# The last block of rows: columns in parts of 384 and 128, squares summed on VectorE, rows stored in halves

## The chip, the cores and the metric

The kernel runs on one core of a Trainium2 chip. The metric is the device time of one execution in microseconds, lower is better. Engines are named as in the profile: PE (TensorE), DVE (VectorE), ACT (ScalarE), POOL (GpSimd), SP (SyncE, which here issues most DMAs).

## The reference

One layer of a hybrid decoder trunk: 512 tokens, model width 1024, float32. What matters here is its last part, the channel mixer's down-projection with its residual, and the final RMSNorm:

```python
u2 = _rmsnorm(h, norm2_g[l])
z = _causal_dwconv(u2 @ w_ffn_up[l], ffn_dw_w[l], ffn_dw_b[l])
h = h + (jax.nn.silu(z[..., :FFN_DIM]) * z[..., FFN_DIM:]) @ w_ffn_down[l]
...
return _rmsnorm(h, final_g)

def _rmsnorm(x, g):
    xf = x.astype(jnp.float32)
    y = xf * lax.rsqrt(jnp.mean(xf * xf, axis=-1, keepdims=True) + EPS)
    return (y * g.astype(jnp.float32)).astype(x.dtype)
```

So each output row needs the mean of the squares of all its 1024 columns before any of it can be scaled.

## The kernel before, in words

**Tiles.** The 512 tokens are four blocks of 128 rows, t = 0 to 3; the 1024 columns are two halves of T = 512, n = 0 and 1. `hres[t, n]` is the residual of one block and half in SBUF. H is 256, P is 128, D is 1024.

**Matmuls.** Every product is split into a high and a low part of each operand, so one product of 128 x 128 weights is three matmuls (`mm3`, lines 448 to 450), high and low parts being `whi`/`wlo` for the weights. The down-projection runs in the function `seven` (a Strassen-like scheme with seven products for two-by-two blocks) over three groups of channel pairs; the third group is the last work of PE. Its steps run in the order a11, a12, s1, n2, s4, n3, a22, each for the two row blocks of one half (i = 0, 1). After a step the result in PSUM is added into `hres` by VectorE (`add`, line 1419). Steps a12, s4, n3 and a22 complete a block and half: a12 completes (0, 0) and (1, 0), s4 completes (0, 1) and (1, 1), n3 completes (2, 1) and (3, 1), a22 completes (2, 0) and then (3, 0). The last to be complete is thus the first half of block 3.

**The last block in two parts.** For (a22, i = 1) in the last group (`fine`), the 512 columns are made in two parts of 256: twelve matmuls into the step's own bank for columns 0 to 256, then twelve into a new bank for 256 to 512. What the old bank holds for the second part from earlier steps is added to `hres` after n3 (line 1441). The two adds, with what they bring about, are in a region in which VectorE and ACT issue in program order; outside such a region a scheduler orders each engine's instructions by the readiness that it expects.

**The final norm.** A `Finish` object for each block collects the pieces. `part` (line 1570 on) is called when a piece of `hres` is complete: ACT squares it and sums the squares into a column of `ss4` (line 1576, two instructions: the pass and the read of the sum), VectorE multiplies it by the gain into `y` (line 1578), and the sums are added up, the first by VectorE with EPS (line 1583), later ones by POOL (line 1585). `scale` adds the last sum (POOL, line 1591) and raises it to the power -1/2 (POOL, line 1592), which gives the factor of each row. `store` scales and writes. For blocks 2 and 3 ACT scales the first 384 columns (line 1598), VectorE the other 640 (line 1599), and SP issues one store of the whole 512 KB block (line 1600). For blocks 0 and 1 ACT scales each half and SP issues two stores of 256 KB (lines 1603, 1604).

**The order around the change.** `last_complete` calls `part`, then `scale` for blocks 2 and 3 when all 1024 columns are there, and `store` for block 2 when the first part of block 3's first half has been handled, for block 3 when the second part has. `last_at` scales and stores blocks 0 and 1 at the start of a22.

Of the kernel before, what the change touches and what calls it, by code (L numbers as in the profile page):

```python
# [12 lines left out]
BF16 = mybir.dt.bfloat16  # L13
U8 = mybir.dt.uint8
AF = mybir.ActivationFunctionType
ALU = mybir.AluOpType

P = 128
D = 1024
T = 512  # L20
# [55 lines left out]
def trunk_layer(ctx: ExitStack, tc: tile.TileContext, a: dict, out: bass.AP):  # L76
    nc = tc.nc
# [23 lines left out]
    def nm(s):  # L101
        return f"{s}_{next(names)}"
# [13 lines left out]
    def small(n, tag):  # L116
        return tp.tile([P, n], F32, tag=tag, name=nm(tag), bufs=4)

    def mm_bank():
        return ps.tile([P, T], F32, tag="mm", name=nm("mm"), bufs=5)  # L120
# [14 lines left out]
    mhalf = cp.tile([P, NT], F32, name="mhalf")  # L135
# [372 lines left out]
    def junk(n):  # L508
        return tp.tile([P, n], BF16, tag="junk", name=nm("junk"), bufs=1)
# [44 lines left out]
    rows = tp.tile([P, P], F32, tag="gain", name=nm("rows"), bufs=1)[0:KT, :]  # L554
# [44 lines left out]
    def root(t):  # L599
        v = small(1, "var")  # L600
        nc.vector.tensor_scalar(v, rs[t], EPS, None, ALU.add)
        rs[t] = tp.tile([P, 1], F32, tag="r1", name=nm("r1"), bufs=NT)
        nc.gpsimd.tensor_tensor(rs[t], v, mhalf[:, :1], ALU.pow)
# [29 lines left out]
    def scale(t):  # L633
        nc.scalar.activation(xs[t], xs[t], AF.Copy, scale=rs[t])
# [95 lines left out]
    acc = mm_bank()  # L730
# [7 lines left out]
    acc = mm_bank()  # L738
# [77 lines left out]
    for k in range(KT):  # L816
# [4 lines left out]
        c = heap()  # L821
# [104 lines left out]
    rows = slice(32, 32 + RANK)  # L926
# [9 lines left out]
    rows = slice(96, 96 + RANK)  # L936
# [165 lines left out]


    H = T // 2

    def f32(x):
        return x.bitcast(F32)

    def token_sums_7(u, src, hi, lo):
# [3 lines left out]
        def part(t, k):  # L1113
            return [u[k][j][:, :, t * H : (t + 1) * H] for j in range(2)]

# [50 lines left out]
    def step_of_two(acts7, acc, step, w, half, opens):  # L1166
        ah, al = acts7[step]
        for k in range(4):
            s = slice(half * T + k * P, half * T + (k + 1) * P)
            mm3(acc[:, :H], (w[0][:, s], w[1][:, s]), (ah[k], al[k]), opens and k == 0, k == 3, not opens)  # L1170

    combined = []

    def two_tiles(name, p, q, acts7, side_bank, at_once=False):

        x, y, z = mm_bank(), side_bank(), side_bank()
        c1, c2 = tmp(), tmp()
        t1, t2 = slice(0, H), slice(H, T)

        def put(c, acc):  # L1180
            nc.scalar.copy(c, acc[:, :H])  # L1181

# [9 lines left out]
        step(z, "a12", w, 1, True)  # L1192
        combine(c1[:, t1], c1[:, t1], z[:, :H], ALU.add)
        yield
# [178 lines left out]
    def seven(name, pairs, acts, complete, at=lambda step, i: None, fine=False):  # L1373

        bank = {"x": [mm_bank(), mm_bank()], "y": [mm_bank(), mm_bank()], "z": [ax_bank(), ax_bank()]}  # L1380
        of = {"a11": "x", "n2": "x", "n3": "x", "a22": "x", "s1": "y", "s4": "y", "a12": "z"}

        into = {
            "a11": (0, 0, ALU.add, False),
            "a12": (0, 0, ALU.add, True),
            "s1": (1, 1, ALU.add, False),
            "n2": (0, 1, ALU.subtract, False),
            "s4": (0, 1, ALU.add, True),
            "n3": (1, 1, ALU.subtract, True),
            "a22": (1, 0, ALU.add, True),  # L1390
        }

        def products(step, i, parts, acc, lo=0, hi=T, opens=False):
            acc = acc[:, lo:hi]
            opens = opens or step in ("a11", "s1", "a12")
            for d, w in parts:
                for j, pair in enumerate(acts[2 * d : 2 * d + 2]):
                    ah, al = (x[:, i * P : (i + 1) * P] for x in pair[step])
                    c = slice(j * T + lo, j * T + hi)

                    read = 2 * d + j == len(acts) - 1
                    mm3(acc, (ah, al), (w[0][:, c], w[1][:, c]), opens and d == 0 and j == 0, read, not opens)

        steps = list(STEPS)
        while steps:
            step, d = steps.pop(0)

            with tc.issue_after(freed.ins) if step == "a22" and not fine else ExitStack():
                parts = [(d, weight(name, (pairs, step, d)))]
                if steps and steps[0] == (step, 1):  # L1410
                    steps.pop(0)
                    parts.append((1, weight(name, (pairs, step, 1))))
            half, n, op, whole = into[step]
            for i in range(2):
                t = 2 * half + i
                acc = bank[of[step]][i]

                def add(n, acc, c=slice(0, T)):
                    done = nc.vector.tensor_tensor(hres[t, n][:, c], hres[t, n][:, c], acc[:, c], op)  # L1419
                    if whole:  # L1420
                        complete(t, n, c)
                    return done

                if fine and (step, i) == ("a22", 1):
                    products(step, i, parts, acc, 0, H)
                    rest = mm_bank()
                    products(step, i, parts, rest, H, T, True)
                    with tc.manual_schedule(engines={ET.DVE, ET.Activation}):
                        add(n, acc, slice(0, H))
                        add(n, rest, slice(H, T))  # L1430
                    continue
                products(step, i, parts, acc)
                if parts[-1][0] == 1:
                    at(step, i)
                    done = add(n, acc)
                    if (step, i) == ("n3", 1):
                        freed = done
                if fine and (step, i) == ("n3", 1):

                    c = slice(H, T)  # L1440
                    nc.vector.tensor_tensor(hres[t, 0][:, c], hres[t, 0][:, c], acc[:, c], ALU.add)


# [1 line left out]
    hres = {}  # L1445
    ss2 = {}
# [48 lines left out]
    ffn_scope, fp = scoped("ffn", 1)  # L1495
# [63 lines left out]
        hi = {"n3": b, "s1": x, "n2": x, "s4": g}  # L1559
        return token_sums_7(u2, {step: src for step in hi}, hi, {"n3": us, "s1": us, "n2": us, "s4": x})  # L1560

    SPLIT = 5 * P

    class Finish:


        def __init__(self, t):
            self.t, self.width = t, 0
            self.y = fp.tile([P, D], F32, tag="kept", name=nm("y"), bufs=2) if t > 1 else None
            self.ss = small(4, "ss4")  # L1570
            self.parts = []

        def part(self, n, c):
            hn = hres[self.t, n][:, c]
            k = len(self.parts)
            nc.scalar.activation(junk(T)[:, c], hn, AF.Square, scale=1.0 / 32.0, accum_out=self.ss[:, k : k + 1])
            y = self.y[:, n * T + c.start : n * T + c.stop] if self.y else tmp() if self.parts else hn
            nc.vector.tensor_tensor(y, hn, gain3[:, n * T + c.start : n * T + c.stop], ALU.mult)
            self.parts.append((n, y))
            self.width += c.stop - c.start  # L1580
            if k == 0:
                self.sum = small(1, "var")
                nc.vector.tensor_scalar(self.sum, self.ss[:, 0:1], EPS, None, ALU.add)
            elif self.width < D:
                nc.gpsimd.tensor_tensor(self.sum, self.sum, self.ss[:, k : k + 1], ALU.add)

        def scale(self):

            k = len(self.parts) - 1
            self.r = small(1, "rstd")  # L1590
            nc.gpsimd.tensor_tensor(self.sum, self.ss[:, k : k + 1], self.sum, ALU.add)
            nc.gpsimd.tensor_tensor(self.r, self.sum, mhalf[:, :1], ALU.pow)

        def store(self):
            rows = slice(self.t * P, (self.t + 1) * P)
            if self.y:
                lo, hi = self.y[:, : D - SPLIT], self.y[:, D - SPLIT :]
                nc.scalar.activation(lo, lo, AF.Copy, scale=self.r)
                nc.vector.tensor_scalar(hi, hi, self.r, None, ALU.mult)
                nc.sync.dma_start(out[rows, :], self.y)  # L1600
                return
            for n, y in reversed(self.parts):
                nc.scalar.activation(y, y, AF.Copy, scale=self.r)
                nc.sync.dma_start(out[rows, n * T : (n + 1) * T], y)

    ends = {}

    def last_complete(t, n, c):
        if t not in ends:
            ends[t] = Finish(t)  # L1610
        ends[t].part(n, c)
        if ends[t].width == D and t > 1:
            ends[t].scale()
        if t == 3 and n == 0:
            ends[2 if c.start == 0 else 3].store()

    def last_at(step, i):

        if (step, i) == ("a22", 0):
            for t in range(2):  # L1620
                ends[t].scale()
            for t in range(2):
                ends[t].store()

    gain3 = None
    banks, values, units = {}, {}, {}
    third = []
    for gi, pairs in enumerate(GROUPS):
        acts = []
        if gi == 0:  # L1630
# [3 lines left out]
            for j, lo in [(j, lo) for lo in (0, H) for j in range(3)]:  # L1634
                late = {(1, 0): (KT - 1, 2), (2, 0): (MID, 3)}.get((j, lo))
                at = {late[0]: lambda t=late[1]: to_channels(normed[t], u2, t)} if late else {}
# [18 lines left out]
        for what, i, *rest in up_plan(gi):  # L1655
            if what == "tile":
                if 0 in rest[0]:
                    banks[i] = (weight("w_up", i), mm_bank())
                wt, acc = banks[i]
# [26 lines left out]
        else:  # L1686
            gain3 = load_gain("final_g")
# [91 lines left out]
```

## Time and profile before

| | |
|---|---|
| median of 3 runs | 821.92 us (821.52, 821.92, 823.87) |
| the profiled execution, its own time | 820.78 us |
| its span | 818.9 us |
| PE busy | 810.3 us (99%), 4287 matmuls |
| DVE busy | 715.6 us (87%) |
| ACT busy | 448.9 us (55%) |
| POOL busy | 148.8 us (18%) |
| chain that ended last | PE 98%, DMA 1%, the rest below 0.5% each |
| granted PE clock | 0.999 |

The span is the time from the first to the last event that the profile shows of the profiled execution; the execution's own time is 1.88 us longer. Times in the rows are us from the start of the span. A row of the timeline has start, duration, engine, line, operation, output <- inputs, shape and, in brackets, the engine's idle time ahead of it with what ended it. A row of the groups has the number of instructions after x, then busy us, the mean of one in ns, and the idle time ahead. A row of the waits has the total in us, how often, and the longest.

### The profile page before, as it was taken

The page shows a single profiled execution, that of the slowest core. Times are in us where ns is not written, and L with a number is a line of the kernel's source. Part 1 is how long each engine was busy: PE and PEld are TensorE (multiplying, and loading weights), DVE is VectorE, ACT ScalarE, POOL GpSimd, SP SyncE. Part 2 cuts the span into 40 slices and gives each one's busy share as a digit, 9 for nine tenths or more (in the row PEclk, how much of TensorE's full clock was granted, in tenths as well). Part 3 has the DMA queues.
Part 4 walks back from the last instruction along what each step waited for, and adds up shares of the span by engine and source line. Part 5 has one row for each costly group of instructions (what it writes and reads, how often), then busy time and mean ns, then how long its engine had stood idle before and what let it go on. Part 6 is the DMA issues. An engine that isn't in the chain of part 4 may idle for free.

```text
span 818.9 us, 11480 instructions
## 1 busy us (share of the span) xinstructions
PE 810.3 (99%) x4287; PEld 700.5 (86%) x4287; DVE 715.6 (87%) x1157; ACT 448.9 (55%) x666; POOL 148.8 (18%) x133
## 2 busy tenths in 40 slices
PE   9999999999999999999999999999999999999996
PEld 7888888888888889999988898898889988899885
DVE  6689999999989699885788889979965999789896
ACT  6643447656663446684444556556435663466554
POOL 2000010001000213633001000230123301622012
PEclk9999999999999999999999999999999999999999
DMA  8355572563532123223657623146642447334662
GB/s 318 104 127 144 148 188 96 130 154 104 120 97 96 49 62 109 88 78 129 206 115 220 187 71 103 52 161 166 134 137 89 144 123 167 104 103 177 158 129 102
DMA packets 30615, 106.25 MB, mean 130 GB/s; under 512 B 3464, under 2 KB 3600, under 8 KB 30560
## 3 DMA queue, kind: packets, MB, share of 16 engines
q1 hardware_dynamic: 24784, 85.34, 30.4%
q0 software_dynamic: 5760, 20.19, 14.4%
q8 instruction: 33, 0.54, 0.3%
q14 instruction: 22, 0.18, 0.1%
q10 hardware_dynamic: 16, 0.00, 0.0%
HBM read 103.42 MB, written 2.10 MB: 129 GB/s over the span
## 4 chain that ended last, share of the span: by engine, by line
PE 98%; DMA 1%; ACT 0%; DVE 0%; POOL 0%; issue 0%; POOLq 0%; SPq 0%; ACTq 0%
PE mm L448 28%; PE mm L449 28%; PE mm L450 28%; PE mm L662 3%; PE ax L450 2%; PE ax L448 2%; PE ax L449 2%; PE ax L1070 1%; PE ax L1072 1%; PE ax L1051 1%; DMA raw<-in_w_v_dram 1%; PE ax L1040 0%; PE ax L529 0%; PE ax L576 0%; PE ax L1085 0%; PE mm L933 0%
## 5 line engine op out<-in xcount | busy, mean ns | idle before, releaser
L448 PE MATMUL mm<-uh,wlo 128*128 128x512 f32 (+1 forms) x672 | 244.4, 364 | 0.0
L449 PE MATMUL mm<-ul,whi 128*128 128x512 f32 (+1 forms) x672 | 242.4, 361 | 0.0
L450 PE MATMUL mm<-uh,whi 128*128 128x512 f32 (+1 forms) x672 | 242.0, 360 | 0.0
L450 PEld LDWEIGHTS mm<-uh,whi 128*128 128x128 f32 x672 | 126.8, 189 | 19.4
L448 PEld LDWEIGHTS mm<-uh,wlo 128*128 128x128 f32 x672 | 127.0, 189 | 18.8
L449 PEld LDWEIGHTS mm<-ul,whi 128*128 128x128 f32 x672 | 127.0, 189 | 18.6
L385 ACT CAST whi<-raw 128x1024 fp32r<-128x1024 f32 x86 | 89.7, 1047 | 54.9 <-PE mm L450 28.2
L356 DVE TENSOR_TENSOR wlo<-raw,whi 128x1024 fp32r<-128x1024 f32 x80 | 93.1, 1171 | 24.4 <-ACT whi L355 20.5
L327 POOL TENSOR_TENSOR raw<-raw,raw 128x512 f32<-128x512 f32 x42 | 67.6, 1610 | 212.8 <-DVE wlo L356 130.7
L390 DVE TENSOR_TENSOR wlo<-raw,whi 128x1024 fp32r<-128x1024 f32 x70 | 92.7, 1327 | 14.1 <-ACT whi L385 14.0
L355 ACT CAST whi<-raw 128x1024 fp32r<-128x1024 f32 x80 | 76.3, 957 | 34.8 <-PE mm L450 27.2
L788 DVE SCALAR_TENSOR_TENSOR c<-h,pp,c 128x255 f32<-128x255 f32 (+14 forms) x120 | 57.5, 479 | 4.0 <-ACT c L784 3.7
L788 DVE SCALAR_TENSOR_TENSOR c<-aside,btmp,c 128x255 f32<-128x255 f32 (+14 forms) x120 | 57.5, 479 | 1.4 <-ACT c L784 1.4
L788 DVE SCALAR_TENSOR_TENSOR aside<-h,pp,aside 128x255 f32<-128x255 f32 (+6 forms) x112 | 53.7, 479 | 0.0
L355 ACT CAST whi<-kept 128x1024 fp32r<-128x1024 f32 (+1 forms) x32 | 31.8, 996 | 31.8 <-DVE kept L310 17.0
L1503 DVE SCALAR_TENSOR_TENSOR tmp<-mm,pp,tmp 128x511 f32<-128x511 f32 (+1 forms) x56 | 41.4, 742 | 4.0 <-ACT tmp L1500 3.9
L356 DVE TENSOR_TENSOR wlo<-kept,whi 128x1024 fp32r<-128x1024 f32 (+1 forms) x32 | 36.8, 1153 | 4.8 <-ACT whi L355 4.7
L1181 ACT COPY tmp<-mm 128x256 f32<-128x256 f32 x48 | 17.7, 368 | 34.4 <-PE mm L450 34.0
L1419 DVE TENSOR_TENSOR hres<-hres,mm 128x512 f32<-128x512 f32 (+1 forms) x49 | 32.3, 671 | 4.7 <-PE mm L450 3.4
L1500 ACT ACTIVATE tmp<-mm,pp 128x512 f32<-128x512 f32 x28 | 21.8, 779 | 19.0 <-PE mm L450 18.9
L387 ACT ACTIVATE wlo<-raw 128x1024 fp32r<-128x1024 f32 x16 | 16.9, 1060 | 22.1 <-PE mm L448 22.1
L1503 DVE SCALAR_TENSOR_TENSOR tmp<-tmp,pp,tmp 128x511 f32<-128x511 f32 (+1 forms) x32 | 27.8, 887 | 0.4
(347 smaller groups left out, 1767.0 us busy)
## 6 DMA issues: line engine op xcount, KB each, us to landing
raw<-in_w_up_dram SPq DMA_DIRECT2D x44, 512.0 KB, 3.5
raw<-in_w_glu_dram SPq DMA_DIRECT2D x16, 512.0 KB, 5.2
raw<-in_w_down_dram SPq DMA_DIRECT2D x15, 512.0 KB, 4.3
kept<-in_w_down_dram POOLq DMA_DIRECT2D x10, 512.0 KB, 5.9
raw<-in_w_v_dram SPq DMA_DIRECT2D x8, 512.0 KB, 5.6
raw<-in_w_qk_dram SPq DMA_DIRECT2D x8, 512.0 KB, 3.4
raw<-in_w_r_dram SPq DMA_DIRECT2D x8, 512.0 KB, 4.6
wlo<-in_w_r_dram POOLq DMA_DIRECT2D x8, 512.0 KB, 8.1
```

The costliest lines, as they stand in the source:

```text
L327: work = nc.gpsimd.tensor_tensor(out, x, y, ALU.add)
L355: nc.scalar.copy(hi, raw)
L356: two_low[:] = [nc.vector.tensor_tensor(lo, raw, hi.bitcast(F32), ALU.subtract)]
L385: nc.scalar.copy(hi, raw)
L390: pace[0] = nc.vector.tensor_tensor(lo, raw, hi.bitcast(F32), ALU.subtract)
L448: nc.tensor.matmul(acc, ll, rh, start=first, stop=False, **kw)
L449: nc.tensor.matmul(acc, lh, rl, start=False, stop=False, **kw)
L450: nc.tensor.matmul(acc, lh, rh, start=False, stop=last, **kw)
L662: nc.tensor.matmul(acc, act, ready[k // 2][wi][:, j], start=first, stop=last)
L788: nc.vector.scalar_tensor_tensor(out[:, j:], x[:, : half_t - j], w, out[:, j:], ALU.mult, ALU.add)
L1419: done = nc.vector.tensor_tensor(hres[t, n][:, c], hres[t, n][:, c], acc[:, c], op)
L1503: nc.vector.scalar_tensor_tensor(z[:, s:], acc[:, : T - s], w[j], z[:, s:], ALU.mult, ALU.add)
```

## The change

The last part of the work, from (a22, i = 1) on, is rearranged.

- Columns 0 to 384 and 384 to 512 take the place of the two parts of 256. The add after n3 that carries over the old bank covers 128 columns rather than 256.
- Block 2: the squares of its second-completed half are summed by VectorE, starting from the sum that is there (`square_onto`, one instruction that multiplies, writes the squares as bfloat16 into a new tile `last`, and sums them onto a start value). POOL's add goes, the power stays. The scaling splits at 768 columns (ACT) and 256 (VectorE), and `store` is called ahead of the two adds of block 3, inside the region in program order.
- Blocks 0 and 1: POOL adds the second sum when the piece is complete, not at a22; the power and the stores stay at a22.
- Block 3: the 384-column part is squared by ACT. The last 128 columns are squared and summed by VectorE onto the first half's sum; a VectorE add joins ACT's sum; POOL makes the power. The gain product of the 384 columns is issued behind that add. VectorE scales columns 512 to 1024, which SP stores (256 KB); VectorE multiplies the last 128 columns by factor and gain in one instruction, ACT scales the 384 columns, and SP stores columns 0 to 512 (256 KB).

```diff
+    CUT = 3 * P
...
                 if fine and (step, i) == ("a22", 1):
-                    products(step, i, parts, acc, 0, H)
+                    products(step, i, parts, acc, 0, CUT)
                     rest = mm_bank()
-                    products(step, i, parts, rest, H, T, True)
+                    products(step, i, parts, rest, CUT, T, True)
                     with tc.manual_schedule(engines={ET.DVE, ET.Activation}):
-                        add(n, acc, slice(0, H))
-                        add(n, rest, slice(H, T))
+                        at("last", i)
+                        add(n, acc, slice(0, CUT))
+                        add(n, rest, slice(CUT, T))
...
-                    c = slice(H, T)
+                    c = slice(CUT, T)
                     nc.vector.tensor_tensor(hres[t, 0][:, c], hres[t, 0][:, c], acc[:, c], ALU.add)
...
-    SPLIT = 5 * P
+    SHARE = 2 * P
...
+        def square(self, n, c, k):
+            nc.scalar.activation(
+                junk(T)[:, c], hres[self.t, n][:, c], AF.Square, scale=1.0 / 32.0, accum_out=self.ss[:, k : k + 1]
+            )
+
+        def square_onto(self, x, total):
+            of = fp.tile([P, T], BF16, tag="last", name=nm("last"), bufs=1)[:, : x.shape[-1]]
+            nc.vector.tensor_tensor_reduce(of, x, x, 1.0 / D, self.sum, ALU.mult, ALU.add, total)
+
+        def gained(self, n, c, y):
+            nc.vector.tensor_tensor(y, hres[self.t, n][:, c], gain3[:, n * T + c.start : n * T + c.stop], ALU.mult)
+
         def part(self, n, c):
+            k = len(self.parts)
+            if self.t == 3 and c.start == CUT:
+                return
             hn = hres[self.t, n][:, c]
-            k = len(self.parts)
-            nc.scalar.activation(junk(T)[:, c], hn, AF.Square, scale=1.0 / 32.0, accum_out=self.ss[:, k : k + 1])
             y = self.y[:, n * T + c.start : n * T + c.stop] if self.y else tmp() if self.parts else hn
-            nc.vector.tensor_tensor(y, hn, gain3[:, n * T + c.start : n * T + c.stop], ALU.mult)
+            if self.t == 2 and k:
+                total = small(1, "total")
+                self.square_onto(hn, total)
+                self.root(total)
+            else:
+                self.square(n, c, k)
+            if c.stop != CUT:
+                self.gained(n, c, y)
             self.parts.append((n, y))
-            self.width += c.stop - c.start
             if k == 0:
                 self.sum = small(1, "var")
                 nc.vector.tensor_scalar(self.sum, self.ss[:, 0:1], EPS, None, ALU.add)
-            elif self.width < D:
-                nc.gpsimd.tensor_tensor(self.sum, self.sum, self.ss[:, k : k + 1], ALU.add)
-
-        def scale(self):
-
-            k = len(self.parts) - 1
+            elif self.t < 2:
+                nc.gpsimd.tensor_tensor(self.sum, self.ss[:, 1:2], self.sum, ALU.add)
+
+        def root(self, total):
             self.r = small(1, "rstd")
-            nc.gpsimd.tensor_tensor(self.sum, self.ss[:, k : k + 1], self.sum, ALU.add)
-            nc.gpsimd.tensor_tensor(self.r, self.sum, mhalf[:, :1], ALU.pow)
+            nc.gpsimd.tensor_tensor(self.r, total, mhalf[:, :1], ALU.pow)
+
+        def end(self):
+
+            last, before = slice(CUT, T), slice(0, CUT)
+            total = small(2, "ss2")
+            self.square_onto(hres[3, 0][:, last], total[:, 0:1])
+            nc.vector.tensor_tensor(total[:, 1:2], total[:, 0:1], self.ss[:, 1:2], ALU.add)
+            self.root(total[:, 1:2])
+            y, r, rows = self.y, self.r, slice(self.t * P, (self.t + 1) * P)
+            self.gained(0, before, y[:, before])
+            nc.vector.tensor_scalar(y[:, T:], y[:, T:], r, None, ALU.mult)
+            nc.sync.dma_start(out[rows, T:], y[:, T:])
+            nc.vector.scalar_tensor_tensor(y[:, last], hres[3, 0][:, last], r, gain3[:, last], ALU.mult, ALU.mult)
+            nc.scalar.activation(y[:, before], y[:, before], AF.Copy, scale=r)
+            nc.sync.dma_start(out[rows, :T], y[:, :T])
 
         def store(self):
             rows = slice(self.t * P, (self.t + 1) * P)
             if self.y:
-                lo, hi = self.y[:, : D - SPLIT], self.y[:, D - SPLIT :]
+                lo, hi = self.y[:, : D - SHARE], self.y[:, D - SHARE :]
                 nc.scalar.activation(lo, lo, AF.Copy, scale=self.r)
                 nc.vector.tensor_scalar(hi, hi, self.r, None, ALU.mult)
                 nc.sync.dma_start(out[rows, :], self.y)
...
-        if ends[t].width == D and t > 1:
-            ends[t].scale()
-        if t == 3 and n == 0:
-            ends[2 if c.start == 0 else 3].store()
+        if t == 3 and c.start == CUT:
+            ends[3].end()
...
             for t in range(2):
-                ends[t].scale()
+                ends[t].root(ends[t].sum)
             for t in range(2):
                 ends[t].store()
+        if step == "last":
+            ends[2].store()
```

More of the change, by code (lines that the diff above doesn't have):

```diff
@@ L1560, in ffn_sums @@
         return token_sums_7(u2, {step: src for step in hi}, hi, {"n3": us, "s1": us, "n2": us, "s4": x})
-    SPLIT = 5 * P
+    SHARE = 2 * P
     class Finish:
         def __init__(self, t):
-            self.t, self.width = t, 0
+            self.t = t
             self.y = fp.tile([P, D], F32, tag="kept", name=nm("y"), bufs=2) if t > 1 else None
```

## The prediction

> **What bounds the kernel now.** I read the table of stages first, then the list of waits of TensorE, then the timeline of the end.
>
> ```profile
> 20.00:809.22 789.22, 789.22 (x4172) 682.17 (x4171) 698.63 (x1127) 432.35 (x638) 142.62 (x111) 1.00 0.44 125
> 809.22:812.25 3.03, 3.03 (x25) 2.82 (x23) 2.62 (x5) 1.61 (x5) 1.04 (x3) 1.00 0.00 0
> 812.25:815.00 2.75, 0.00 (x0) 0.00 (x0) 1.47 (x4) 1.35 (x4) 0.94 (x3) 1.00 0.46 191
> 815.00:818.90 3.90, 0.00 (x0) 0.00 (x0) 0.00 (x0) 0.00 (x0) 0.00 (x0) 0.74 0.33 134
> ```
>
> The columns are the stage, its length, then the busy time of PE, PEld, DVE, ACT and POOL. From 20 us on, PE is busy in all of its stage, at a granted clock of 1.00, up to 812.25. Its only idle waits lie in the first stage:
>
> ```profile
> PE mm L568 <- DVE ones L541: 1.1, 1, 1.1
> PE mm L662 <- ACT h L589: 0.8, 1, 0.8
> ```
>
> So no engine beside PE can shorten what lies ahead of 812.25. The edit reaches the last matmuls and the 818.9 - 812.25 = 6.65 us behind them. This is that end:
>
> ```profile
> 809.41 0.69 DVE L1419 TENSOR_TENSOR hres<-hres,mm 128x512 f32<-128x512 f32 x1 [0.42 <-PE mm L450]
> ...
> 811.97 0.28 PE L450 MATMUL mm<-whi,ah 128*128 128x256 f32 x1
> 812.33 0.41 DVE L1419 TENSOR_TENSOR hres<-hres,mm 128x256 f32<-128x256 f32 x1
> ...
> 812.83 0.42 ACT L1576 ACTIVATE junk<-hres 128x256 bf16<-128x256 f32 x1 [0.36 <-DVE hres L1419]
> 813.16 0.19 ACT L1576 ACTIVATION_READ_ACCUMULATOR junk<-hres 128x1 f32 x1
> 813.49 0.19 POOL L1591 TENSOR_TENSOR var<-ss,var 128x1 f32<-128x1 f32 x1 [1.03 <-ACT junk L1576]
> 813.75 0.55 POOL L1592 TENSOR_TENSOR rstd<-var,mhalf 128x1 f32<-128x1 f32 x1
> 814.34 0.61 ACT L1598 ACTIVATE y<-y,rstd 128x384 f32<-128x384 f32 x1 [0.99 <-POOL rstd L1592]
> 814.34 0.55 DVE L1599 TENSOR_SCALAR y<-y,rstd 128x640 f32<-128x640 f32 x1 [1.14 <-POOL rstd L1592]
> 814.98 0.33 SPq L1600 DMA_DIRECT2D out_dram<-y  x1
> ```
>
> One chain: the last product ends at 811.97 + 0.28 = 812.25, then come residual add, squares, POOL's add, POOL's power (the root), the scaling, and at 814.98 the issue of one 512 KB store.
>
> **The store.** Its price and that of a half are in the table of DMA issues:
>
> ```profile
> out_dram<-y SPq DMA_DIRECT2D x2, 512.0 KB, 2.6
> out_dram<-tmp SPq DMA_DIRECT2D x2, 256.0 KB, 2.1
> ```
>
> The old one lands at 814.98 + 2.6 = 817.58; 1.3 us of closing follow, which I take as fixed. The new last store is of 256 KB: 2.1 from its issue, a gain of 0.5. It is issued behind its twin, though, on SP's queue (an issue takes 0.33), so they share the wire; if the pair costs what 512 KB do, it is 2.6. I take 2.1, the row of its own size, and keep 2.6.
>
> **Durations.** The groups kept apart by shape:
>
> ```profile
> L1419 DVE TENSOR_TENSOR hres<-hres,mm 128x512 f32<-128x512 f32 x47 | 31.4, 681 | 4.7 <-PE mm L450 3.4 <-DMA hres<-in_x_dram 1.2
> L1419 DVE TENSOR_TENSOR hres<-hres,mm 128x256 f32<-128x256 f32 x2 | 0.8, 418 | 0.0
> L1578 DVE TENSOR_TENSOR y<-hres,gain 128x512 f32<-128x512 f32 x3 | 2.1, 689 | 0.1
> L1578 DVE TENSOR_TENSOR y<-hres,gain 128x256 f32<-128x256 f32 x2 | 0.9, 428 | 0.1
> L1467 DVE SCALAR_TENSOR_TENSOR un<-hres,rstd,gain 128x512 f32<-128x512 f32 x8 | 5.6, 747 | 1.8 <-POOL rstd L500 1.8
> L1599 DVE TENSOR_SCALAR y<-y,rstd 128x640 f32<-128x640 f32 x2 | 1.1, 554 | 1.3 <-POOL rstd L1592 1.1
> L1583 DVE TENSOR_SCALAR var<-ss 128x1 f32<-128x1 f32 x4 | 0.6, 151 | 1.1 <-ACT junk L1576 1.1
> L1576 ACT ACTIVATE junk<-hres 128x512 bf16<-128x512 f32 x7 | 4.4, 628 | 5.5 <-DVE hres L1419 5.5
> L1576 ACT ACTIVATE junk<-hres 128x256 bf16<-128x256 f32 x2 | 0.8, 418 | 0.8 <-DVE hres L1419 0.8
> L1576 ACT ACTIVATION_READ_ACCUMULATOR junk<-hres 128x1 f32 x9 | 1.7, 187 | 0.0
> L1603 ACT ACTIVATE tmp<-tmp,rstd 128x512 f32<-128x512 f32 x2 | 1.4, 720 | 1.1 <-POOL rstd L1592 1.1
> L1598 ACT ACTIVATE y<-y,rstd 128x384 f32<-128x384 f32 x2 | 1.2, 616 | 1.0 <-POOL rstd L1592 1.0
> ```
>
> On straight lines through two widths: residual add 128 columns 0.29, 384 columns 0.55; gain product 128 columns 0.30, 384 columns 0.56; tensor_scalar 512 columns 0.47, 256 columns 0.31 (through 0.15 at one column); scalar_tensor_tensor of 128 columns 0.30 + (0.75 - 0.69) = 0.36; ACT scaling of 768 columns 0.72 + 2 x 0.10 = 0.92. The old 256-column square holds ACT for 0.52 with its read (812.83 to 813.35); one of 384 columns 0.52 + 0.11 = 0.63.
>
> **The sum of squares on VectorE.** No VectorE instruction of this trace writes a sum out. Its stream is a two-input pass: 0.69 at 512 columns, 0.30 at 128. For the sum's read I bound 0 to 0.19, the latter from ACT's read, and take 0.19, its only kin. Nothing in the rows excludes a slower pass. The Trainium skill's page "VectorE: DVE Perf Modes", section "Two Vector instructions with no wait between them", says that an op that also writes its accumulator is two instructions, the main one and a read. With that rule the sum below stands; without it, it would be 0.19 shorter for token block 2 and 0.10 for the last, 822.0 in place of 822.3.
>
> **Who holds up POOL's power.** The change puts a gain product on VectorE right behind each sum from which POOL makes a root. Look at VectorE and POOL together:
>
> ```profile
> 803.00 0.68 DVE L1578 TENSOR_TENSOR tmp<-hres,gain 128x512 f32<-128x512 f32 x1
> 803.60 1.22 DVE L356 TENSOR_TENSOR wlo<-kept,whi 128x1024 fp32r<-128x1024 f32 x1
> ...
> 803.05 0.68 POOL L1591 TENSOR_TENSOR var<-ss,var 128x1 f32<-128x1 f32 x1 [1.90 <-ACT junk L1576]
> 803.81 1.42 POOL L1592 TENSOR_TENSOR rstd<-var,mhalf 128x1 f32<-128x1 f32 x1
> ...
> 811.27 0.55 POOL L1592 TENSOR_TENSOR rstd<-var,mhalf 128x1 f32<-128x1 f32 x1
> 811.30 0.43 DVE L1578 TENSOR_TENSOR y<-hres,gain 128x256 f32<-128x256 f32 x1
> ```
>
> POOL's add takes 0.19 alone and 0.68 when a VectorE product of two tiles began before it; it ends at 803.73, just behind the product (803.68). The power takes 0.55 alone and 1.42 at 803.81, ending at 805.23, 0.41 after the VectorE pass that began before it (804.82). At 811.27 the power began first, and lost nothing. In the new order the product follows the sum on the same engine at once, while POOL hears of the sum some 0.08 later (the old add to the power: 813.68 to 813.75). So both powers come second, and each costs the product's length + 0.41 in place of 0.08 + 0.55: 0.69 + 0.41 = 1.10 for block 2, 0.56 + 0.41 = 0.97 at the end. The price is 0.47 and 0.34. The other bound is no price, where POOL gets in first. The Trainium skill, "SBUF — State Buffer", section "Who interferes with whom", states the mechanism: a VectorE instruction with two SBUF inputs and a GpSimd one that reads SBUF exclude each other, and the earlier holds the other up to its end. By the rule the sum is 822.3, without it 821.4; the rows above agree with it.
>
> **The matmuls.** The 24 products of 256 columns become 12 of 384 and 12 of 128:
>
> ```profile
> 808.99 0.39 PE L450 MATMUL mm<-whi,ah 128*128 128x512 f32 x1
> 809.22 0.28 PE L448 MATMUL mm<-whi,al 128*128 128x256 f32 x1
> ...
> 173.63 1.06 PE L1040 MATMUL ax<-q,k 128*128 128x128 f32 x8
> ...
> L1040 PE MATMUL ax<-q,k 128*128 128x128 f32 x32 | 4.2, 275 | 0.0
> ```
>
> A 512-column product takes 0.23 from start to start (808.99 to 809.22), a 256-column one (811.97 - 809.22) / 23 = 0.12. On that line 384 columns take 0.173 and 128 take 0.067: 2.08 + 0.80 = 2.88, as before. The first part is there 0.6 later (last start 809.22 + 11 x 0.173 = 811.12, end 811.46, add from 811.50), the second at the old 812.3. But no product of this kind with 128 columns is in the trace. The nearest rows are the plain f32 ones of L1040: eight records for four matmuls, (1.06 - 0.275) / 7 = 0.11 a record, 0.22 a matmul (1.06 is seven steps and one length of 0.275). Bounds: 0.067 and 0.22. I take the low end, since it continues the line of the same kind of product; up to about 0.12 the difference is hidden, as the sum shows.
>
> **The sum.** Block 2's add ends at 809.41 + 0.69 = 810.10.
> - Sum of squares, 512 columns, from 810.14: 0.69 + 0.19, to 811.02. Gain product to 811.73, power to 812.14. Before, ACT's squares ran beside the product, and the power ended at 811.82.
> - Now block 2's scaling is issued ahead of the last block's adds, in an order fixed for VectorE and ACT. The 256 columns on VectorE wait for the root: 812.18 to 812.49. Behind them queue both residual adds; ACT's 768 columns run to 813.10, and the 384-column square queues behind. Block 2's own store goes out about 813.1 rather than 812.50, and lands before the last one is issued.
> - Adds: 384 columns to 813.04, 128 columns to about 813.33. So the second part, there at 812.3, waits 0.7 for VectorE: this is the cover of slower products.
> - Sum of squares, 128 columns: 813.36 + 0.30 + 0.19 = 813.85. ACT's square: 813.10 + 0.63 = 813.73, just hidden. The small add on VectorE (0.15) ends at 814.02; POOL's add (0.19) is gone.
> - Gain product of 384 columns to 814.60, power to 815.01.
> - VectorE: 512 columns 815.05 to 815.52, store 1 issued at 815.55. Then 128 columns to about 815.88; ACT's 384 columns end at 815.67. Store 2 is issued at about 815.9, as SP is free at 815.88.
> - Landing 815.9 + 2.1 = 818.0, against 817.58: **0.4 us later**.
>
> The span goes to 819.3, and the profiled execution from 820.78 to 821.2. The three runs shown have a median of 821.92, 1.14 above the profiled one; the difference laid on the median gives 822.3.
>
> Edits that cost nothing: the residual add ahead of the last products (L1441) shrinks from 256 to 128 columns, 0.13 less, and VectorE idles 0.42 behind it anyway (the bracket at 809.41); POOL's adds for blocks 0 and 1 move a stage earlier, ahead of the same roots, whose stores are out long before 809. Without that cover each is worth 0.2 at most.
>
> **The rivals.**
> - *The narrow products are slow.* If a 128-column product costs 0.22, PE's last one starts at 811.30 + 11 x 0.22 = 813.7 and ends some 0.25 later; the last add begins at about 814.0 rather than 813.04. The chain behind it is the same: 0.4 + 1.0 = 1.4 slower, **823.3**. It decides from 0.12 a product on, where the 0.7 of cover ends. For it: the only 128-column rows cost that much. Against: they are another kind of product, and 512 to 256 columns shows no such step.
> - *POOL gets in first.* Both powers run at 0.55. Block 2's root is there at 811.65, its scaling starts behind the gain product at 811.76; ACT ends it at 812.68 and the square at 813.31; small add to 813.47, power to 814.1, store 2 at 815.0, landing at 817.1: **821.4**, 0.5 faster. For it: 811.27. Against: 803.05 and 803.81, where VectorE began first, as here.
> - *The halves land together.* With 2.6 the end is 0.5 later than in my sum: **822.8**. For it: both issues lie within 0.4 us. Against: the stores of L1604 came in pairs too and took 2.1 each.
> - *Everything overlaps.* VectorE free when the second part arrives, POOL in first and the sum's read free: add 812.3 to 812.6, sum to 812.9, small add to 813.1, power to 813.7, store 2 at 814.6: landing at 816.7, 0.9 faster, **821.0**. Against: the queue behind block 2's root stands in program order.
>
> **How the numbers follow.** My forecast has a chance of 0.47 (own range 821.8 to 822.8), slow products 0.23, POOL first 0.15, late landing 0.10, the full gain 0.05. A change smaller than 0.3% (2.5 us) can't be told from none here: the three runs themselves lie 2.35 apart. Every case stays inside it; slow products with a late landing come to 1.9. Outside are only a sum of squares several times dearer than its kin, or a shift of the median: 0.07 slower, 0.03 faster, 0.90 same. The range, 820.9 to 823.8, holds the cases from 821.0 to 823.3 and half a microsecond of the median's own spread.
>
> **What would show it.** Right: a power of about 1 us or more twice behind VectorE's products, the 384-column add starting only behind block 2's scaling (about 812.5, not 811.5), the last store issued near 815.9. Wrong: powers of 0.55; 128-column products further apart than 0.12; a VectorE sum much longer than 0.9 or 0.5; a second store that takes 2.6. It falls altogether if PE's stage ahead of 809 changes its length.

## The result and the profile after

The changed kernel takes 827.0 us (median of 6 runs, beside 821.72 of 6 runs of the kernel before); the forecast was 822.3, with a range of 820.9 to 823.8. One of the six, the one that was profiled, ran at a granted clock of 0.753 and took 1012.53 us; the ratio, 1.0056 with a 95% interval of 1.0034 to 1.0078, is that of the means without it, and the profile shown here is that of experiment e1. There the changed kernel was taken again: 825.61 beside 821.13, ratio 1.0055 (1.0042 to 1.0068). So it is 0.55% slower, some 4.5 us, where 0.4 us was forecast. The profiled execution of e1 took 825.28, with a span of 823.6 against 818.9.

The head of its page (engine, busy time, share, instructions):

```profile
span 823.6 us, 11478 instructions
PE 815.4 (99%) x4287; PEld 701.9 (85%) x4287; DVE 715.2 (87%) x1162; ACT 447.9 (54%) x662; POOL 146.7 (18%) x130
```

PE is busy for 815.4 us instead of 810.3, with the same number of matmul records, 4287. Its list of waits:

```profile
PE mm L568 <- DVE ones L541: 1.1, 1, 1.1
PE mm L662 <- ACT h L589: 0.6, 1, 0.6
```

They are the two waits of before, the second 0.6 in place of 0.8. So PE waits for nothing new: its matmuls themselves take longer. Where, the timeline of PE shows. First the kernel before, with the step of 512 columns ahead of the last one (start, duration):

```profile
804.68 0.39 PE L449 MATMUL mm<-wlo,yh 128*128 128x512 f32 x1
...
808.99 0.39 PE L450 MATMUL mm<-whi,ah 128*128 128x512 f32 x1
809.22 0.28 PE L448 MATMUL mm<-whi,al 128*128 128x256 f32 x1
```

From 804.68 to 809.22 are 20 starts: 0.227 each. (A row's duration, 0.39, is longer than that: the rows of neighbouring products overlap.) The same twenty in the changed kernel (e1):

```profile
808.95 0.39 PE L449 MATMUL mm<-wlo,yh 128*128 128x512 f32 x1
...
813.37 0.40 PE L450 MATMUL mm<-whi,ah 128*128 128x512 f32 x1
813.60 0.34 PE L448 MATMUL mm<-whi,al 128*128 128x384 f32 x1
```

From 808.95 to 813.60: 0.2325 each. The last step, the only one whose products the change touches, begins 813.60 - 809.22 = 4.38 us later than before. That is nearly all of the 4.7 us by which the span grew, and it came about in work in which the order of instructions, their shapes and their waits are the old ones.

Which matmuls are slower, the groups kept apart by shape tell (count, busy us, mean ns). Before:

```profile
L450 PE MATMUL mm<-uh,whi 128*128 128x512 f32 x488 | 190.0, 389 | 0.0
L450 PE MATMUL mm<-whi,sh 128*128 128x512 f32 x66 | 25.7, 389 | 0.0
L450 PE MATMUL mm<-h,whi 128*128 128x512 f32 x64 | 24.9, 390 | 0.0
...
L450 PE MATMUL mm<-c,whi 128*128 128x256 f32 x24 | 6.8, 283 | 0.0
```

The changed kernel (e1):

```profile
L450 PE MATMUL mm<-uh,whi 128*128 128x512 f32 x488 | 190.2, 390 | 0.0
L450 PE MATMUL mm<-whi,sh 128*128 128x512 f32 x66 | 26.1, 395 | 0.0
L450 PE MATMUL mm<-h,whi 128*128 128x512 f32 x64 | 25.3, 395 | 0.0
...
L450 PE MATMUL mm<-c,whi 128*128 128x256 f32 x24 | 6.8, 281 | 0.0
```

Products with `uh` stay; those of 512 columns with `sh` or `h` take 5 to 6 ns longer, and those of 256 columns, with `c`, don't. Over all groups of 512 columns the slower ones are those with h, c, ch, sh, sl, yh, yl, ah or al as an operand: 958 products whose means rose by 3 to 7 ns, 4.7 us together, about the 4.38 by which the last step is late. What these tiles share, all but `ch`, is their place. In the built programs the change's new one-column tile `total`, of which the pool keeps four buffers of 32 bytes per partition, moves every tile allocated behind it by 128 bytes (`h` from byte 124,672 to 124,800, `c` from 177,920 to 178,048, `yh` from 127,744 to 127,872, `al` from 165,632 to 165,760), while the weights `whi` and `wlo` and the tiles `uh` and `ul` lie ahead of it and stay. So 830 of the 958 have a moved operand. The other 128, those with `ch`, have none: `ch` lies on the other side of the memory and stays where it was. But each product with `c`, which moved, stands between two with `ch`. The other new tile, `last`, has 1,024 bytes and lies behind all tiles of its pool.

Last, the end in e1, from the timelines of VectorE, POOL, PE and SP (in part, and without ACT):

```profile
813.80 0.69 DVE L1420 TENSOR_TENSOR hres<-hres,mm 128x512 f32<-128x512 f32 x1 [0.63 <-PE mm L450]
814.52 0.75 DVE L1582 CUSTOM_DVE_ANT_0 last<-hres,var 128x512 bf16<-128x512 f32 x1
815.20 0.08 DVE L1582 DVE_READ_ACCUMULATOR2_ANT total<- 128x1 f32 x1
815.20 0.69 DVE L1585 TENSOR_TENSOR y<-hres,gain 128x512 f32<-128x512 f32 x1
815.36 0.93 POOL L1610 TENSOR_TENSOR rstd<-total,mhalf 128x1 f32<-128x1 f32 x1 [5.96 <-DVE total L1582]
815.71 0.22 PE L448 MATMUL mm<-whi,al 128*128 128x128 f32 x1
...
816.88 0.27 PE L450 MATMUL mm<-whi,ah 128*128 128x128 f32 x1
816.33 0.35 DVE L1632 TENSOR_SCALAR y<-y,rstd 128x256 f32<-128x256 f32 x1 [0.44 <-POOL rstd L1610]
816.60 0.88 DVE L1420 TENSOR_TENSOR hres<-hres,mm 128x384 f32<-128x384 f32 x2
817.52 0.35 DVE L1582 CUSTOM_DVE_ANT_0 last<-hres,var 128x128 bf16<-128x128 f32 x1
817.79 0.08 DVE L1582 DVE_READ_ACCUMULATOR2_ANT ss<- 128x1 f32 x1
817.98 0.16 DVE L1617 TENSOR_TENSOR ss<-ss,ss 128x1 f32<-128x1 f32 x1
818.05 0.55 DVE L1585 TENSOR_TENSOR y<-hres,gain 128x384 f32<-128x384 f32 x1
818.22 0.80 POOL L1610 TENSOR_TENSOR rstd<-ss,mhalf 128x1 f32<-128x1 f32 x1 [1.92 <-DVE ss L1617]
819.05 0.49 DVE L1621 TENSOR_SCALAR y<-y,rstd 128x512 f32<-128x512 f32 x1 [0.44 <-POOL rstd L1610]
819.56 0.33 SPq L1622 DMA_DIRECT2D out_dram<-y  x1
820.00 0.37 SPq L1625 DMA_DIRECT2D out_dram<-y  x1
```

Against the forecast, with the 4.38 us by which the last step begins later taken off:

| | forecast | e1 less 4.38 |
|---|---|---|
| block 2: add ends | 810.10 | 810.11 |
| sum of squares read | 811.02 | 810.90 |
| power ends | 812.14 | 811.91 |
| block 3: both adds end | 813.33 | 813.10 |
| sum of squares read | 813.85 | 813.49 |
| power ends | 815.01 | 814.64 |
| last store issued | 815.9 | 815.62 |
| span ends | 819.3 | 819.22 |

### The profile page after: what moved, and what is told of

It is laid out like the page before. It is cut to its first block, busy times and chain, and to the rows that moved or that the text cites. A ratio compares the mean times of both kernels' runs of the same rounds, so it can differ in the third digit from the quotient of the medians.

```text
span 1010.6 us, 11478 instructions
## 1 busy us (share of the span) xinstructions
PE 1003.1 (99%) x4287; PEld 768.9 (76%) x4287; DVE 721.6 (71%) x1162; ACT 450.7 (45%) x662; POOL 137.9 (14%) x130
## 4 chain that ended last, share of the span: by engine, by line
PE 99%; issue 0%; DVE 0%; POOL 0%; POOLq 0%; DVEq 0%
PE mm L450 28%; PE mm L448 28%; PE mm L449 28%; PE mm L662 3%; PE ax L450 2%; PE ax L449 2%; PE ax L448 2%; PE ax L1070 1%; PE ax L1051 1%; PE ax L1072 1%; PE ax L576 0%; PE mm L568 0%; PE ax L1040 0%; PE ax L529 0%; PE ax L1085 0%
## 5 line engine op out<-in xcount | busy, mean ns | idle before, releaser
L448 PE MATMUL mm<-uh,wlo 128*128 128x512 f32 (+1 forms) x672 | 283.5, 422 | 0.0
L449 PE MATMUL mm<-ul,whi 128*128 128x512 f32 (+1 forms) x672 | 280.5, 417 | 0.0
L450 PE MATMUL mm<-uh,whi 128*128 128x512 f32 (+1 forms) x672 | 279.6, 416 | 0.0
L450 PEld LDWEIGHTS mm<-uh,whi 128*128 128x128 f32 x672 | 136.3, 203 | 40.8
L449 PEld LDWEIGHTS mm<-ul,whi 128*128 128x128 f32 x672 | 136.7, 203 | 40.1
L448 PEld LDWEIGHTS mm<-uh,wlo 128*128 128x128 f32 x672 | 135.7, 202 | 40.4
L356 DVE TENSOR_TENSOR wlo<-raw,whi 128x1024 fp32r<-128x1024 f32 x80 | 92.8, 1165 | 52.5 <-ACT whi L355 52.3
L390 DVE TENSOR_TENSOR wlo<-raw,whi 128x1024 fp32r<-128x1024 f32 x70 | 86.4, 1234 | 26.5 <-ACT whi L385 26.3
L327 POOL TENSOR_TENSOR raw<-raw,raw 128x512 f32<-128x512 f32 x42 | 60.4, 1437 | 290.7 <-DVE wlo L356 194.4
L1420 DVE TENSOR_TENSOR hres<-hres,mm 128x512 f32<-128x512 f32 (+2 forms) x49 | 32.6, 673 | 21.8 <-PE mm L450 21.6
L450 PE MATMUL mm<-whi,sh 128*128 128x512 f32 x66 | 30.6, 464 | 0.0
```

What stands on the lines that cost most here:

```text
L327: work = nc.gpsimd.tensor_tensor(out, x, y, ALU.add)
L356: two_low[:] = [nc.vector.tensor_tensor(lo, raw, hi.bitcast(F32), ALU.subtract)]
L390: pace[0] = nc.vector.tensor_tensor(lo, raw, hi.bitcast(F32), ALU.subtract)
L448: nc.tensor.matmul(acc, ll, rh, start=first, stop=False, **kw)
L449: nc.tensor.matmul(acc, lh, rl, start=False, stop=False, **kw)
L450: nc.tensor.matmul(acc, lh, rh, start=False, stop=last, **kw)
```

## The experiments

They ran in three groups (e1 to e4; e5 to e8; e9 to e12), each beside its own runs of the kernel before: medians 821.13, 821.21 and 821.12, of 21 to 25 runs.

**e1_after.** The changed kernel as it is.

> The changed kernel as it is, for a profile at full granted clock. Theory 'end' (queue behind block 2's root, narrow products): PE's last step still begins near 809.2 us, and the time from there to the end grows from 9.7 to 13 us or more. Theory 'placement' (the new small tile moves the heap, conv and ffn tiles by 128 bytes and makes VectorE, ScalarE or TensorE slower on them) and theory 'own sum' (a VectorE instruction that sums makes the whole program slower): the last step begins 3 to 5 us later, at 812 to 814, and the end behind it is 9.7 to 10.5 us.

825.61, ratio 1.0055 (1.0042 to 1.0068). The loss is there again, and the profile above shows PE's products as its place.

**e2_after_unmoved.** The whole change, but its new small tile takes a name whose buffers exist already, so that no other tile moves.

```diff
-                total = small(1, "total")
+                total = small(1, "r1")
```

> The changed kernel with block 2's sum in a small tile that is there already, so that no other tile moves. Placement: the 4 to 5 us go, 821.5 to 822.5. End, own sum: as the changed kernel, 825 to 828.

821.58, ratio 1.0002 (0.9993 to 1.0010), span 819.4. The groups are those of before:

```profile
L450 PE MATMUL mm<-whi,sh 128*128 128x512 f32 x66 | 25.7, 389 | 0.0
L450 PE MATMUL mm<-h,whi 128*128 128x512 f32 x64 | 24.9, 390 | 0.0
```

So the rearranged end is not what costs 4.5 us.

**e3_before_moved.** The kernel before with the small tile and nothing else; nothing writes or reads it.

```diff
+            if t == 2:
+                small(1, "total")
```

> The kernel before with an unused small tile, which moves the heap, conv and ffn tiles by the same 128 bytes; every instruction stays. Placement: 825 to 828. End, own sum: 821.7 as before.

825.11, ratio 1.0043 (1.0031 to 1.0055), span 823.4. The old kernel becomes nearly as slow as the new one by a tile that no instruction uses:

```profile
L450 PE MATMUL mm<-whi,sh 128*128 128x512 f32 x66 | 26.0, 395 | 0.0
L450 PE MATMUL mm<-h,whi 128*128 128x512 f32 x64 | 25.3, 395 | 0.0
```

**e4_before_sum.** The kernel before, with VectorE instead of ACT summing the squares of block 2's second half.

```diff
+            if self.t == 2 and k:
+                nc.vector.tensor_tensor_reduce(
+                    junk(T)[:, c], hn, hn, 1.0 / D, 0.0, ALU.mult, ALU.add, self.ss[:, k : k + 1]
+                )
+            else:
...
```

> The kernel before, with the squares of block 2's second half summed by VectorE instead of ScalarE; nothing moves, and the end stays in its old order. Own sum: 825 or more. Placement: 821.7. End: 821.7 to 822.5.

821.66, ratio 1.0005 (0.9996 to 1.0015), span 819.2. The new kind of instruction costs nothing outside of its own place. With e2, which keeps the whole rearranged end and the tile `last`, and e3, this leaves the shift of the tiles.

**e5_moved_64 and e6_moved_256.** The kernel before with an unused tile of 64 bytes in place of 128, or of 256 (`[P, 64]`).

```diff
+            if t == 2:
+                tp.tile([P, 16], F32, tag="total", name=nm("total"), bufs=1)
```

> The kernel before with heap, conv and ffn tiles moved by 64 bytes. Theory 'grid' (a matmul operand that does not start at a multiple of 256 bytes slows products of 512 columns from 227 to about 232 ns): 824 to 826. Theory 'distance' (what counts is the distance of the two operands, modulo 256): 824 to 826 too. Theory 'half step' (only an odd multiple of 128 is bad): 821 to 822.

> The same with 256 bytes. Grid, distance, half step: 821 to 822, products at 227 ns. Theory 'crowding' (any shift, or any tile more, costs): 825.

64 bytes: 826.29, ratio 1.0059 (1.0042 to 1.0076). 256 bytes: 821.13, ratio 0.9995 (0.9986 to 1.0004). In the groups, e5:

```profile
L450 PE MATMUL mm<-whi,sh 128*128 128x512 f32 x66 | 26.1, 395 | 0.0
L450 PE MATMUL mm<-h,whi 128*128 128x512 f32 x64 | 25.1, 393 | 0.0
```

and e6:

```profile
L450 PE MATMUL mm<-whi,sh 128*128 128x512 f32 x66 | 25.7, 389 | 0.0
L450 PE MATMUL mm<-h,whi 128*128 128x512 f32 x64 | 24.9, 389 | 0.0
```

So it isn't moving as such, nor the room that was taken: a shift by 256 is free, by 64 and 128 not.

**e7_all_moved.** Is it the place of a tile on a grid of 256 bytes, or its distance from the other operand? The pad ahead of all tiles on that side, weights included, grows by 128 bytes.

```diff
-PADS = (416, 992, 768)
+PADS = (544, 992, 768)
```

> The kernel before with every tile of the left side moved by 128 bytes, the weights too, so that the distance between weights and activations stays. Distance: 821 to 822. Grid, half step: the products with the first projections' activations slow down as well (some 1,500 more of 512 columns at 5 ns), 830 or more.

821.45, ratio 1.0002 (0.9993 to 1.0012): when both operands move together the time stays, and the products with `uh` and `sh` keep their 389 ns, though none of their operands starts at a multiple of 256 bytes any more. So the grid isn't what counts; how the operands lie to each other is. This run holds a second answer: `ch` lies on the other side of the memory and did not move, so its distance from the weights is no longer what it was. By its tile (minimum, median, maximum in ns), before, then e7, then e1:

```profile
L448 PE MATMUL mm<-ch,wlo x64: 389/389/396, 370.1 to 430.4; 128*128 128x512 f32 x64
L448 PE MATMUL mm<-ch,wlo x64: 392/393/394, 370.2 to 430.7; 128*128 128x512 f32 x64
L448 PE MATMUL mm<-ch,wlo x64: 392/397/404, 371.0 to 432.2; 128*128 128x512 f32 x64
```

The median rises by 4 ns in e7, where the distance changed. It rises by 8 in e1, where neither `ch` nor the weights moved. So the distance between a product's own two operands isn't the whole rule. The longest stretch of these products, 108 in a row of which every third has `c` and the others `ch`, says the same. From start to start they take 0.2269 us before (406.60 to 431.11), 0.2334 in e1 (407.73 to 432.94) and 0.229 in e7 (406.63 to 431.35). By the distance of a product's own operands e1 would lose on one in three and e7 on two in three; but e1 loses as if on all, and e7 as if on little more than one in three. What a neighbouring product has to do with it is not shown.

**e8_ffn_moved.** Only the tiles of the last stage move by 128 bytes: a pad at the head of their pool.

```diff
+    fp.tile([P, P // 4], F32, tag="pad", name=nm("pad"), bufs=1)
```

> The kernel before with only the ffn tiles moved by 128 bytes; heap and conv tiles stay. The placement theory gives the part of the 4.4 us that the moved kernel's trace shows behind 563 us, 2.2: 823.0 to 823.6, products with the seven-step activations at 232 ns and those with heap tiles at 227.

823.06, ratio 1.0023 (1.0013 to 1.0032), span 821.8. The groups: `sh`, which moved, is slow, `h`, which didn't, is not.

```profile
L450 PE MATMUL mm<-whi,sh 128*128 128x512 f32 x66 | 26.0, 394 | 0.0
L450 PE MATMUL mm<-h,whi 128*128 128x512 f32 x64 | 24.9, 389 | 0.0
```

The loss is about in proportion: sh, sl, yh, yl, ah and al make 198 + 132 + 120 = 450 of the 958 slower products, 47%, and 0.23% of the time is 42% of e1's 0.55%.

**e9_short_chain and e12_short_chain_384.** With no tile moved, could a shorter end be had than the change's? Parts of 256 again (384 in e12), POOL joins the earlier sums ahead of time, VectorE's sum of the last part ends the total, and no gain product stands behind it: VectorE scales and multiplies one half in one instruction. Block 2 too is scaled and stored in halves, behind the first add of block 3. Block 3's halves go out on two queues.

```diff
+            total = small(1, "r1")
+            self.square_onto(hres[3, 0][:, CUT:T], total)
+            self.root(total)
...
+            nc.scalar.activation(y[:, T:], y[:, T:], AF.Copy, scale=r)
+            queue.dma_start(out[rows, T:], y[:, T:])
+            nc.vector.scalar_tensor_tensor(y[:, :T], hres[self.t, 0], r, gain3[:, :T], ALU.mult, ALU.mult)
+            nc.sync.dma_start(out[rows, :T], y[:, :T])
```

> Nothing moves. Parts of 256 and 256; block 3's first sums are joined ahead of the last part, so that POOL's power follows VectorE's sum with no add between and no product beside it; a half of the rows is scaled by ScalarE, the other multiplied by factor and gain in one VectorE instruction; the two stores go out on two queues. Theory 'the end is a sum of its steps': last add to about 813.1 (in a run whose last step begins at 809.5), sum to 813.6, power of 0.55 to 814.2, both halves to 815.0, landing at 817.2, that is 0.6 us ahead of the kernel before: 820.5. Rival 'the end is bound elsewhere' (stores, POOL): 821.1 to 821.6.

> The same with parts of 384 and 128. If narrow products cost 0.11 rather than 0.067, the last part is there 0.5 later and its add and sum are 0.25 shorter: 0.2 to 0.3 us slower than with 256 and 256. If the narrow part pays: up to 0.25 faster.

e9: 820.99, ratio 0.9996 (0.9987 to 1.0005); e12: 821.36, ratio 1.0007 (0.9998 to 1.0016). Neither beats the kernel before. Counted from the start of the last step (809.68, before 809.22) e9's last store goes out after 5.57 us, against 5.76: the chain is shorter, but by 0.2 only. In e9 the power is undelayed and both stores are issued at once:

```profile
813.88 0.55 POOL L1610 TENSOR_TENSOR rstd<-r,mhalf 128x1 f32<-128x1 f32 x1 [1.06 <-DVE r L1582]
...
815.22 0.40 ACTq L1622 DMA_DIRECT2D out_dram<-y  x1
815.25 0.33 SPq L1624 DMA_DIRECT2D out_dram<-y  x1
```

but its table of DMA issues (KB each, median us from issue to landing) has the half at the price of the whole block:

```profile
out_dram<-y ACTq DMA_DIRECT2D x1, 256.0 KB, 2.7
```

So this store, with its twin 0.03 us behind, takes as long as one of 512 KB does (2.6 before); whether ACT's queue has a part in it was not tried. In e1, 0.44 apart and both on SP's queue, they took 2.3 (median):

```profile
out_dram<-y SPq DMA_DIRECT2D x2, 256.0 KB, 2.3
```

**e10_product_first.** e2, with the gain product of 384 columns ahead of the last sum, so that POOL's last power finds VectorE free.

```diff
+            self.gained(0, before, self.y[:, before])
             self.square_onto(hres[3, 0][:, last], total[:, 0:1])
...
-            self.gained(0, before, y[:, before])
```

> The changed kernel with nothing moved, and block 3's gain product of 384 columns issued ahead of the last sum rather than behind it. Theory 'the product holds up POOL': the last power takes 0.55 to 0.63 in place of 0.80. Rival 'this power is slow by itself': 0.80 stays. The end: 0.1 to 0.3 later, as the product now stands in the chain.

One run: 821.13, span 819.4. The power and the last store:

```profile
814.38 0.55 POOL L1610 TENSOR_TENSOR rstd<-ss,mhalf 128x1 f32<-128x1 f32 x1 [2.27 <-DVE ss L1618]
...
815.91 0.37 SPq L1625 DMA_DIRECT2D out_dram<-y  x1
```

The power takes 0.55 in place of 0.80, so the hold by VectorE's product is real; but the product now stands ahead of the sum, and the store goes out no earlier: 6.50 us behind the start of the last step (809.41), and 6.40 in e2 (815.88 - 809.48).

**e11_add_first.** e2, with the 384-column add ahead of block 2's scaling.

```diff
-                        at("last", i)
                         add(n, acc, slice(0, CUT))
+                        at("last", i)
                         add(n, rest, slice(CUT, T))
```

> The changed kernel with nothing moved, and block 2's scaling and store issued behind the 384-column add. Theory 'the queue behind block 2's root costs up to 0.7' : that add begins near 811.8 rather than 812.5 and the last store goes out 0.3 or more earlier. Rival 'the narrow products are late anyway' (last one ends near 813.0): the last store moves by less than 0.1.

One run: 821.12, span 819.4. The adds of VectorE:

```profile
811.81 0.56 DVE L1420 TENSOR_TENSOR hres<-hres,mm 128x384 f32<-128x384 f32 x1
...
813.10 0.29 DVE L1420 TENSOR_TENSOR hres<-hres,mm 128x128 f32<-128x128 f32 x1 [0.47 <-PE mm L450]
...
815.91 0.37 SPq L1625 DMA_DIRECT2D out_dram<-y  x1
```

The first add starts early, as meant, but the second has to wait for PE (the bracket), whose narrow products are done only then. The last store goes out 6.40 us behind the start of the last step (809.51), as in e2. So the queue behind block 2's root costs nothing here, as PE would hold the second add anyway.

## Why the prediction was wrong

**The step that failed** is the first conclusion: "So no engine beside PE can shorten what lies ahead of 812.25. The edit reaches the last matmuls and the 818.9 - 812.25 = 6.65 us behind them." That no other engine is in PE's way was right, before and after. But it doesn't follow that PE's own products keep their length: 789 us of them were taken as fixed. The change moved an operand of 830 of them, and these and the 128 with `ch` among them became longer, by 4.38 us up to the last step. The new tiles had no price in the sum at all. Nor did any rival hold this; only the last sentence on what would make it wrong named PE's stage ahead of 809, with no mechanism. The runs put the place of the operands to each other there instead: e3 has it without the change, e2 the change without it, e6 and e7 the shift without the loss.

**The sum of the end was right.** It said 0.4 later. From the start of the last step to the end of the span are 9.68 us before (809.22 to 818.9) and 10.0 in e1 (813.60 to 823.6): 0.3. In e2, where the shift is gone, they are 9.92 (809.48 to 819.4), and the ratio of 1.0002 fits 0.4 later as well as none. So the change without its shift is what was forecast, by its rows; by the run times alone it can't be told from no change. That the end came out to 0.1 us is partly luck: terms that were too dear and terms that were too cheap made up for each other, as the next points say.

**POOL held up by VectorE**: right. The powers took 0.93 and 0.80 and ended at 816.29 and 819.02, 0.40 and 0.42 behind the products that end at 815.89 and 818.60 (forecast: 0.41). They end earlier than forecast since the sums did. Against the old way, 0.08 and then 0.55, the hold costs 0.38 and 0.25 (1.01 and 0.88 from the end of the sum to that of the power), where 0.47 and 0.34 were in the sum.

**VectorE's sum**: the pass was under-sized for 512 columns (0.75 for 0.69) and for 128 (0.35 for 0.30), the read over-sized: 0.08, where ACT's 0.19 was taken. The Trainium skill's rule ("VectorE: DVE Perf Modes", "Two Vector instructions with no wait between them") that such an op is two instructions agrees with the trace: pass and read stand in it as two rows.

**The narrow products**: mis-sized, and hidden all the same. The 128-column ones are (816.88 - 815.71) / 11 = 0.106 apart, between the bounds of 0.067 and 0.22, and nearer to the first than the rival of slow products would have it. The forecast's cover reached to about 0.12. In e11, where the cover is taken away, the wait for them is visible at once.

**The two halves**: 2.3 from issue to landing, between the 2.1 taken and the 2.6 kept as a bound. The last rows of the table above show that the earlier issue pays for that. The pairs of L1604 that the prediction set against this rival were further apart than the new halves, 0.61 us (803.62 and 804.23), so they could not decide it.

**The range** of 820.9 to 823.8 was made from costs of the end only. Since all of them lie within 1.9 us, the chance of 0.90 for no change was only as good as the assumption that nothing else moves. For a larger change it named a much dearer sum of squares or a shift of the median, and neither is what came.

## What to carry to other kernels

Where PE is busy all the time, a change can cost time without an instruction of its own: any new or resized tile moves the ones behind it, and here 128 bytes cost 4.4 us, while the rearranged work cost about 0.3. So before and after an edit compare the addresses of matmul operands and the start-to-start time of untouched products; if the latter changed, look at the addresses before you look at the edit. Here a name whose buffers existed already was free (e2), and so was a shift by 256 bytes (e6); other shifts have to be measured.

## What the runs showed of the hardware

A 512-column product of these operands takes 0.227 us from start to start in the kernel before. With the activations moved by 128 bytes against the weights it takes 0.2325, and a move by 64 lengthens the rows as much (395 and 393 ns in e5). A move by 256 does not (389 in e6), and neither does a move of both by 128 (e7). Products of 256 columns show nothing of it (`c` moved, 283 and 281 ns).

It isn't a rule of single products: those with `ch` become longer in e1 with both operands in their old place. Nor does e7 part the distance of the two operands from that to the other tiles of their side, as all of these moved together. What collides stays open: no wait is recorded, and a load of weights (0.19 of each 0.23 us) runs beside every product before and after. It was not tried whether other distances (32 or 192 bytes) cost as much, or whether some distance is better than that of before.

The Trainium skill says in "TensorE: Matmul & The Clock Gate", section "Step-by-step: what each phase is for": "Loading the next tile's weights doesn't steal SBUF read bandwidth from the running matmul." No run here shows whether the loss comes from these two reads: if it does, that sentence does not hold for these operands; if it is of another kind, the sentence may stand. What the runs show is that a product's time depends on the addresses, by (0.2325 - 0.227) / 0.227 = 2.4%, at granted clocks of 0.998 and 0.999.
